# Modulation ahead of the splits, a boundary left to the scheduler, six split chunks, and shorter row steps in a two-block transformer kernel

## The chip, the cores and the metric

The kernel runs on one core of one Trainium2 chip. What counts is the device time of one execution in microseconds. The engines named here are PE (TensorE, the matrix multiplications), ACT (ScalarE), DVE (VectorE), POOL (GpSimd) and SP (SyncE, which here only starts transfers). A kernel is timed in several runs and the median is given; one more execution is recorded by the hardware profiler, and all rows below come from that one.

## The reference

Two networks run one behind the other on a residual stream `x` of 512 tokens by 1024 features, in float32. The first block is an attention mixer of two kinds of heads, a cross attention to a memory of 256 rows, and a SwiGLU MLP. The second has two layers, and its input norms are modulated by a shift and a scale that come from a condition vector:

```python
# block 1
x = x + rms_norm(mixer(rms_norm(x, g_mix_pre)), g_mix_post)
x = x + rms_norm(memory_cross_attention(rms_norm(x, g_mem_pre), m, ...), g_mem_post)
x = x + rms_norm(swiglu(rms_norm(x, g_ffn_pre), w_gate_up, w_down), g_ffn_post)
# block 2: layer 0 has the mLSTM mixer, layer 1 latent attention (MLA)
def modulate(h, shift, scale):
    return h * (1 + scale[:, None, :]) + shift[:, None, :]
def sqrelu_mlp(h, w1, w2):
    return jnp.square(jax.nn.relu(h @ w1)) @ w2
```

Shift, scale and the gates of each layer are rows of the product of the condition vector with a large matrix, `ada_w`; MLA has such rows of its own (`kv_ada_w`). Every norm divides by the root of the mean square over the 1024 features.

## The kernel before

**Products.** Each float32 operand is split into a high and a low part, and a product is three matmuls into the same bank: high by high (L447), high by low (L448) and low by high (L449). Activations are split by `parts` (high on ACT L626, low on DVE L627), weight chunks on ACT L307 or L317 and DVE L308 or L318. A hidden chunk of the relu² MLPs, after the first block of columns, is made with the seven products of Winograd's scheme (`wino`, L510, DVE lines 524 to 534), then goes through relu, square (L1458, L1459) and `parts`.

**Boundaries.** At the end of a stage `boundary` walks over the four token tiles. A tile's product is accumulated (DVE L1358) and multiplied by the gain (L1363), its mean square taken on ACT (L579) and turned into a factor on POOL (`rstd`, L568 and L562), the residual stream updated (DVE L648), its mean square taken again, and the stream scaled for the next stage (`scaled`, ACT L598). `put` then transposes the scaled tile on PE (L608), applies the modulation where there is one (`mod`: two 128x128 pieces of each half on DVE L616, two on ACT L619), and splits. Between these steps the products of the next tiles and, at the end, the first products of the next stage, given by `first`, are issued. The whole is inside `ordered()`, in which PE, ACT, DVE and POOL keep the order of the program text. Outside it a list scheduler with a simulated timeline sets each engine's order; a region can be given a priority (`hot`).

**MLP.** `mlp` goes over blocks of hidden chunks. In the last block it sets a cap of `lc` split weight chunks in advance (`cap`), loads the two weight groups of the block, and leaves its products to `boundary`. Split chunks live in buffers of a pool of `s8` = 14; a buffer comes free when the last product that reads it has run.

**Rows in the background.** A generator makes the modulation rows beside the main work. A half row of 512 columns takes eight loads of 128x512 from `ada_w` (`araw`, POOL L868, four buffers), eight multiply-adds on DVE (L863), one fold (L872), a split, and one matmul with ones that sums over partitions (the row sum, L881). The row is scaled (L898), stored to memory (`arow`, POOL L201) and, as a column, loaded again (`cols_steps`, POOL L381) and transposed on PE (L386). Each step of the generator takes in two loads and issues two. Main work advances it: `step(cost)` takes the cost from a counter, 0.65 for a product, 0.34 for a Winograd product, and when the counter falls below zero it is set to `pace` again and the generator takes one step.

```python
        self.pace -= cost
        if self.pace < 0 and not self.quiet:
            self.pace = BUF["pacb" if self.late else "pace"]
            self.step_bg()
```

**Start.** `self.before` names, by the number of the weight chunk, the loads of x tiles (`get`) that are issued on SP ahead of that chunk's load.

## Time and profile before

| | |
|---|---|
| median of three runs | 2026.44 us (2026.16 to 2029.08) |
| the profiled execution, its own time | 2028.55 us |
| its span | 2026.5 us |
| mean granted TensorE clock | 0.985 |
| PE busy | 1943.2 us (96%), 10738 matmuls |
| DVE busy | 1373.4 us (68%) |
| ACT busy | 1073.1 us (53%) |
| POOL busy | 355.6 us (18%) |
| traffic | 242.01 MB, mean 119 GB/s |

The profiled execution is 2.1 us above the median, and 2.05 us of it lie outside the span. The rows that follow further down come from four views: the waits (who waits for whom, in sum), the timeline of an engine (start, length, engine, line, operation, output and inputs, number of instructions in the row, and in brackets the idle time ahead of it with what ended it), windows (busy time by engine in a stretch, with the granted clock, where 1.00 is 2.4 GHz and 0.50 is 1.2), and the instructions of one line. `L447` is line 447 of the kernel before.

### The profile page before, as it was taken

How to read it: one execution, taken by the hardware profiler on the slowest of the kernel's cores; microseconds unless marked ns; L12 is line 12 of the kernel's file. 1: busy time of each engine (PE TensorE's matmuls, PEld its weight loads, DVE VectorE, ACT ScalarE, POOL GpSimd, SP SyncE). 2: the span in 40 equal slices, each digit the busy share in tenths (PEclk: the TensorE clock that was granted, in tenths of full speed). 3: DMA queues.
4: the chain of work that ended last, by engine and by line, in shares of the span. 5: the costliest groups of instructions: out<-in, count | busy, mean ns of one | idle time of the engine just before them, and what ended most of it. 6: DMA issues, size and time to landing. Idle time of an engine off the chain costs nothing. (4 is left out here: it accounts for less than half of the span.)

```text
span 2026.5 us, 29742 instructions
## 1 busy us (share of the span) xinstructions
PE 1943.2 (96%) x10738; PEld 1663.4 (82%) x10738; DVE 1373.4 (68%) x2689; ACT 1073.1 (53%) x2355; POOL 355.6 (18%) x711
## 2 busy tenths in 40 slices
PE   7999999999999999899999899998889989999997
PEld 5888988878888888678888788888687879989996
DVE  5756655856666665576866888898568747657665
ACT  6767775545353243556446464455465556545543
POOL 1331111201122211121323221222120012000000
PEclk9999999999999999999999999999999999999999
DMA  6322342523465554153442354565243212233321
GB/s 198 89 79 65 113 136 74 187 73 115 136 208 177 161 172 116 52 169 101 154 135 84 110 162 138 185 188 165 62 114 94 84 63 73 73 114 105 104 85 62
DMA packets 175251, 242.01 MB, mean 119 GB/s; under 512 B 20108, under 2 KB 117537, under 8 KB 175105
## 3 DMA queue, kind: packets, MB, share of 16 engines
q1 hardware_dynamic: 150704, 170.53, 27.2%
q0 software_dynamic: 24400, 69.60, 11.5%
q8 instruction: 84, 1.38, 0.3%
q14 instruction: 63, 0.51, 0.1%
HBM read 237.88 MB, written 2.20 MB: 118 GB/s over the span
## 5 line engine op out<-in xcount | busy, mean ns | idle before, releaser
L447 PE MATMUL ps<-s,s 128*128 128x512 f32 (+4 forms) x2276 | 863.0, 381 | 26.7 <-ACT s L626 25.1
L448 PE MATMUL ps<-s,s 128*128 128x512 f32 (+4 forms) x2276 | 851.6, 375 | 2.8 <-DVE s L627 1.9
L449 PE MATMUL ps<-s,s 128*128 128x512 f32 (+4 forms) x2276 | 849.7, 375 | 1.5 <-DVE s L627 1.4
L447 PEld LDWEIGHTS ps<-s,s 128*128 128x128 f32 (+2 forms) x2276 | 432.0, 190 | 105.9 <-ACT s L626 31.0
L449 PEld LDWEIGHTS ps<-s,s 128*128 128x128 f32 (+2 forms) x2276 | 431.2, 190 | 83.2 <-DVE s L627 5.2
L448 PEld LDWEIGHTS ps<-s,s 128*128 128x128 f32 (+2 forms) x2276 | 432.3, 190 | 79.1 <-DVE s L627 4.0
L510 PEld LDWEIGHTS ps<-s,s 128*128 128x128 f32 x2184 | 261.8, 188 | 6.7 <-DVE u L526 4.5
L510 PE MATMUL ps<-s,s 128*128 128x256 f32 x2184 | 263.7, 281 | 3.6 <-DVE u L526 3.6
L307 ACT ACTIVATE s<-raw 128x512 fp32r<-128x512 f32 x277 | 157.8, 622 | 143.2 <-PE ps L449 97.9
L308 DVE TENSOR_TENSOR s<-raw,s 128x512 fp32r<-128x512 f32 x277 | 190.3, 726 | 57.0 <-ACT s L307 55.7
L863 DVE SCALAR_TENSOR_TENSOR u<-araw,cond,u 128x512 f32<-128x512 f32 x224 | 167.3, 747 | 24.2 <-DMA araw<-in_ada_w 15.4
L317 ACT ACTIVATE s<-raw,cols_all 128x256 fp32r<-128x256 f32 (+1 forms) x305 | 143.5, 546 | 66.5 <-PE ps L449 29.8
L318 DVE SCALAR_TENSOR_TENSOR s<-raw,cols_all,s 128x256 fp32r<-128x256 f32 (+1 forms) x305 | 147.6, 538 | 39.3 <-ACT s L317 38.7
L868 POOL DMA_DIRECT2D araw<-in_ada_w x192 | 104.0, 542 | 338.0 <-DVE u L863 289.2
L627 DVE TENSOR_TENSOR s<-u,s 128x512 fp32r<-128x512 f32 x126 | 87.0, 700 | 79.4 <-ACT s L626 56.7
L626 ACT ACTIVATE s<-u 128x512 fp32r<-128x512 f32 x126 | 77.6, 625 | 63.8 <-PE ps L449 31.9
L568 POOL TENSOR_SCALAR sm<-sm,sm 128x1 f32<-128x1 f32 x34 | 10.5, 307 | 527.5 <-ACT junk L579 527.4
L341 ACT ACTIVATE s<-raw 128x512 fp32r<-128x512 f32 x104 | 62.7, 621 | 72.7 <-PE ps L449 37.6
L627 DVE TENSOR_TENSOR s<-ps,s 128x512 fp32r<-128x512 f32 (+3 forms) x100 | 59.1, 606 | 42.4 <-ACT s L626 35.0
L341 ACT ACTIVATE s<-u 128x512 fp32r<-128x512 f32 x78 | 48.7, 624 | 66.8 <-DVE u L345 36.4
L342 DVE TENSOR_TENSOR s<-raw,s 128x512 fp32r<-128x512 f32 x104 | 70.7, 683 | 15.4 <-ACT s L341 15.1
L1358 DVE TENSOR_TENSOR u<-ps,u 128x512 f32<-128x512 f32 x80 | 53.9, 685 | 34.3 <-PE ps L449 33.6
(261 smaller groups left out, 2162.9 us busy)
## 6 DMA issues: line engine op xcount, KB each, us to landing
raw<-in_mlp_w SPq DMA_DIRECT2D x128, 512.0 KB, 3.8
araw<-in_ada_w POOLq DMA_DIRECT2D x192, 256.0 KB, 3.5
raw<-in_w_gate_up SPq DMA_DIRECT2D x44, 512.0 KB, 4.1
raw<-in_w_in SPq DMA_DIRECT2D x24, 512.0 KB, 4.2
raw<-in_a_w_in SPq DMA_DIRECT2D x24, 512.0 KB, 3.8
raw<-in_w_down SPq DMA_DIRECT2D x22, 512.0 KB, 3.7
raw<-in_w_mem_kv SPq DMA_DIRECT2D x16, 512.0 KB, 3.6
araw<-in_kv_ada_w POOLq DMA_DIRECT2D x32, 256.0 KB, 4.0
```

What stands on the lines that cost most here:

```text
L307: A.activation(hi[:, sl, cl], src[:, sl, cl], AF.Copy)
L308: f.tensor_tensor(out=lo[:, sl, cl], in0=src[:, sl, cl], in1=hi[:, sl, cl].bitcast(F32), op=ALU.subtract)
L317: A.activation(hi[:, i, :], src[:, i, :], AF.Copy, scale=g)
L318: V.scalar_tensor_tensor(out=lo[:, i, :], in0=src[:, i, :], scalar=g, in1=hi[:, i, :].bitcast(F32), op0=ALU.mult, op1=ALU.subtract)
L341: A.activation(hi, x, AF.Copy)
L447: self.nc.tensor.matmul(ps, lhsT=ah, rhs=bh, start=first and i == 0, stop=False)
L448: self.nc.tensor.matmul(ps, lhsT=ah, rhs=bl, start=False, stop=False)
L449: self.nc.tensor.matmul(ps, lhsT=al, rhs=bh, start=False, stop=last and i == n - 1)
L510: nc.tensor.matmul(ps, lhsT=l[:, k, :], rhs=m[:, k, :], start=first and k == e == 0, stop=k == 3 and e == 2, skip_group_check=True)
L627: self.nc.vector.tensor_tensor(out=lo, in0=x, in1=hi.bitcast(F32), op=ALU.subtract)
L863: V.scalar_tensor_tensor(out=acc, in0=raws.pop(j), scalar=vec[:, j:j + 1], in1=acc, op0=ALU.mult, op1=ALU.add)
L868: nc.gpsimd.dma_start(out=raws[j], in_=ws[:, j, :])
```

## The change

Six things are edited. In `put`, with a modulation, both halves of a tile are modulated first, in place of the scaled tile, and then both are split. `boundary` gets an argument `fixed`; without it the region isn't held in program order, and the scalings, puts and reductions run with the scheduler's priority `hb` = 300. The first relu² MLP, in front of MLA, uses `fixed=False`; the last MLP, which has no next stage, stays. `lc` goes from 7 to 6, `pace` and `pacb` from 2.0 to 1.9. A column is transposed five generator steps after its load instead of three. At the start the x tiles are loaded before weight chunks 1 and 3 instead of 2 and 4.

```diff
-BUF = dict(... pace=2.0, pacb=2.0, ... lc=7, ...)
+BUF = dict(... pace=1.9, pacb=1.9, ... lc=6, ...)
...
-        for _ in range(3):
+        for _ in range(5):
             yield None
...
     def put(self, ys, h, k, t, mod=None):
+        todo = []
         for y, cw in ys:
...
-            hi, lo = h.blk(k, n, tt(t))
             if mod:
                 g, sh = mod
-                y = self.u2((P, n, P))
+                y = y.rearrange("p (n c) -> p n c", c=P)
...
                 ps = y
+            todo.append((k, n, ps))
+            k += n
+        for k, n, ps in todo:
+            hi, lo = h.blk(k, n, tt(t))
             self.parts(hi, lo, ps)
-            k += n
...
-    def boundary(self, y_of, nxt, first, late=(1, 1, 2)):
+    def boundary(self, y_of, nxt, first, late=(1, 1, 2), fixed=True):
...
-        with self.ordered():
+        hot = nullcontext if fixed else lambda: self.hot("hb")
+        with self.ordered() if fixed else nullcontext():
...
-                    if n == 4 and nxt and t >= 2:
+                    if n == 4 and nxt and t >= 2 and fixed:
                         self.put(*pend.pop(t - 2))
-                if nxt and t >= 1:
-                    scaled(t - 1)
-                rs[t] = a(t, ys, ss)
+                with hot():
+                    if nxt and t >= 2 and not fixed:
+                        self.put(*pend.pop(t - 2))
+                    if nxt and t >= 1:
+                        scaled(t - 1)
+                    rs[t] = a(t, ys, ss)
             if nxt:
-                i = -1
+                if not fixed:
+                    with hot():
+                        scaled(NT - 1)
                 for i, need in enumerate(first):
-                    if i == late[0]:
+                    if fixed and i == late[0]:
                         scaled(NT - 1)
-                    for n, t in ((1, NT - 2), (2, NT - 1)):
-                        if i == late[n]:
-                            self.put(*pend.pop(t))
+                    for t in sorted(pend):
+                        if t <= need if not fixed else i >= late[t - 1]:
+                            with hot():
+                                self.put(*pend.pop(t))
...
-        self.before = {2: [lambda: get(1)], 4: [lambda: get(2), lambda: get(3)], 6: [biases]}
+        self.before = {1: [lambda: get(1)], 3: [lambda: get(2), lambda: get(3)], 6: [biases]}
...
-    def mlp(self, blocks, up, w_down, g, nxt, first, ready=None, caps=None):
+    def mlp(self, blocks, up, w_down, g, nxt, first, ready=None, caps=None, fixed=True):
...
-                self.boundary(y_of, nxt, first)
+                self.boundary(y_of, nxt, first, fixed=fixed)
...
-        self.mlp(BUF['mb'], up, self.a["mlp_w2_2"][l], g, nxt, first, ready, BUF['mc'])
+        self.mlp(BUF['mb'], up, self.a["mlp_w2_2"][l], g, nxt, first, ready, BUF['mc'], fixed=nxt is None)
```

How this moves instructions, at three places. In the rows a name ends in two numbers, the buffer and the tile's own number, and from `boundary` on the lines of the changed kernel are a few higher (L608 becomes L609, L626 L629, L881 L891).

The first place is PE at the end of the first relu² MLP's Winograd products. Before, `ps_14007` is the first tile's product of the last block, `s_2498_13975` its last hidden chunk, and `ps_13831` and `ps_13833` belong to the last Winograd products:

```order
L448 MATMUL ps_14007<-s_2489_13903,s_2453_13669 128x512
L510 MATMUL ps_13831<-s_2021_10571,s_2473_13795 128x256 x12
L449 MATMUL ps_14007<-s_2489_13903,s_2454_13670 128x512
L510 MATMUL ps_13833<-s_2064_10938,s_2474_13814 128x256 x12
L447 MATMUL ps_14007<-s_2493_13942,s_2498_13975 128x512
L448 MATMUL ps_14007<-s_2493_13942,s_2498_13975 128x512
L449 MATMUL ps_14007<-s_2493_13942,s_2498_13975 128x512
```

With the change, `ps_14094`, `ps_14119`, `ps_14157` are products of the last block (two tiles, two column halves), `ps_13946` belongs to the last Winograd product, and the last hidden chunk, `s_2520_14073`, is first used 17 matmuls after this `L510` row:

```order
L449 MATMUL ps_14157<-s_2510_13975,s_2486_13801 128x512
L447 MATMUL ps_14157<-s_2514_14010,s_2485_13800 128x512
L510 MATMUL ps_13946<-s_2106_11099,s_2500_13927 128x256 x12
L449 MATMUL ps_14094<-s_2514_14010,s_2486_13801 128x512
L447 MATMUL ps_14094<-s_2514_14010,s_2485_13800 128x512
L448 MATMUL ps_14094<-s_2514_14010,s_2485_13800 128x512
L448 MATMUL ps_14119<-s_2518_14063,s_2485_13800 128x512
L449 MATMUL ps_14119<-s_2518_14063,s_2486_13801 128x512
L449 MATMUL ps_14094<-s_2514_14010,s_2486_13801 128x512
L447 MATMUL ps_14119<-s_2518_14063,s_2485_13800 128x512
L448 MATMUL ps_14119<-s_2518_14063,s_2485_13800 128x512
L449 MATMUL ps_14119<-s_2518_14063,s_2486_13801 128x512
```

The four products of the first two tiles now stand among and behind the last Winograd matmuls, where one product stood.

The second place is the boundary of that MLP with MLA, on ACT. `x_10_91` and `x_11_92` are the third and the fourth tile of the residual stream, and `u_2589_14368` (before) and `u_2611_14458` (after) the first MLA tile. Before:

```order
L598 ACTIVATE u_2575_14308<-x_10_91,sm_14220 128x512
L598 ACTIVATE u_2576_14310<-x_10_91,sm_14220 128x512
L579 ACTIVATE junk_14319,sm_14318<-x_11_92 128x1024
L317 ACTIVATE s_2562_14261<-raw_13994,cols_2283_12462 128x384
L317 ACTIVATE s_2568_14279<-raw_14003,cols_2283_12462 128x384 x2
L317 ACTIVATE s_2569_14288<-raw_14264,cols_2283_12462 128x384
L579 ACTIVATE junk_14371,sm_14370<-u_2589_14368 128x256
L598 ACTIVATE u_2594_14377<-u_2589_14368,sm_14375 128x256
L598 ACTIVATE u_2598_14389<-x_11_92,sm_14323 128x512
L598 ACTIVATE u_2599_14391<-x_11_92,sm_14323 128x512
L626 ACTIVATE s_2537_14155<-ps_14393 128x4x128
```

With the change:

```order
L598 ACTIVATE u_2595_14395<-x_10_91,sm_14307 128x512
L598 ACTIVATE u_2596_14397<-x_10_91,sm_14307 128x512
L317 ACTIVATE s_2589_14374<-raw_14372,cols_2123_11223 128x384 x2
L317 ACTIVATE s_2647_14622<-raw_14437,cols_2123_11223 128x384 x2
L317 ACTIVATE s_2649_14639<-raw_14455,cols_all_1926 128x512 x2
L579 ACTIVATE junk_14406,sm_14405<-x_11_92 128x1024
L629 ACTIVATE s_2565_14284<-ps_14538 128x4x128
L629 ACTIVATE s_2567_14288<-ps_14543 128x4x128
L317 ACTIVATE s_2650_14648<-raw_14496,cols_all_1926 128x512 x2
L598 ACTIVATE u_2603_14412<-x_11_92,sm_14410 128x512
L598 ACTIVATE u_2604_14414<-x_11_92,sm_14410 128x512
L579 ACTIVATE junk_14461,sm_14460<-u_2611_14458 128x256
```

The two scalings of `x_11_92` stood behind the mean square of the MLA tile and stand ahead of it now. On POOL `row_14325` is the MLA bias row that DVE's L1693 adds to that tile, and `sm_14323` the factor of `x_11_92`; before:

```order
L568 TENSOR_SCALAR sm_14312<-sm_14267,sm_14303 128x1
L562 TENSOR_TENSOR sm_14314<-sm_14312,mhalf_80 128x1
L568 TENSOR_SCALAR sm_14321<-sm_14318 128x1
L562 TENSOR_TENSOR sm_14323<-sm_14321,mhalf_80 128x1
L585 DMA row_14325<-arow_4175 128x320
L585 DMA row_14583<-arow_4175 128x384
L568 TENSOR_SCALAR sm_14373<-sm_14370 128x1
```

With the change the load, now `row_14416`, is in the boundary behind the mLSTM mixer:

```order
L562 TENSOR_TENSOR sm_10540<-sm_10538,mhalf_80 128x1
L568 TENSOR_SCALAR sm_10614<-sm_10374,sm_10605 128x1
L562 TENSOR_TENSOR sm_10616<-sm_10614,mhalf_80 128x1
L585 DMA row_14416<-arow_4175 128x320
L568 TENSOR_SCALAR sm_10623<-sm_10620 128x1
L562 TENSOR_TENSOR sm_10625<-sm_10623,mhalf_80 128x1
```

It moved by 110 places of POOL's order, out of the MLA boundary.

The third place is PE in the first block of the first relu² MLP, where `u_2055_10873` (before) and `u_2121_11174` (after) are the row loaded back as a column. Before:

```order
L448 MATMUL ps_10803<-s_2021_10571,s_1989_10414 128x256
L449 MATMUL ps_10803<-s_2021_10571,s_1989_10414 128x256
L881 MATMUL ps_10855<-u_2052_10828,onesr_78 128x512
L386 MATMUL ps_10911<-ident_66,u_2055_10873 128x8
L447 MATMUL ps_10979<-s_1995_10449,s_2044_10785 128x512
L448 MATMUL ps_10979<-s_1995_10449,s_2044_10785 128x512
```

With the change:

```order
L448 MATMUL ps_11142<-s_2035_10600,s_2079_10923 128x512
L449 MATMUL ps_11142<-s_2035_10600,s_2080_10924 128x512
L891 MATMUL ps_11159<-u_2099_11079,onesr_78 128x512
L447 MATMUL ps_11143<-s_2034_10591,s_2079_10923 128x512
...
L448 MATMUL ps_11143<-s_2062_10825,s_2102_11090 128x512
L449 MATMUL ps_11143<-s_2062_10825,s_2102_11090 128x512
L386 MATMUL ps_11221<-ident_66,u_2121_11174 128x8
L447 MATMUL ps_11239<-s_2063_10842,s_2079_10923 128x512
L448 MATMUL ps_11239<-s_2063_10842,s_2079_10923 128x512
```

Between the row sum and the transposition stood nothing, and now 36 matmuls stand there.

## Rows read from the trace of the kernel before

**Rows 1.** Waits of PE: engine, line, releaser: us in total, times, longest.

```profile
PE ps L447 <- ACT s L626: 25.1, 16, 3.9
PE ps L608 <- ACT u L598: 18.3, 10, 7.5
PE ps L386 <- DMA u<-arow: 5.8, 2, 4.7
PE ps L1824 <- DVE u L1833: 4.9, 3, 2.5
```

**Rows 2.** Timeline of PE, last block, first relu² MLP: start us, us, [idle <-releaser].

```profile
1407.22 0.50 PE L881 MATMUL ps<-u,onesr 128*128 128x512 f32 x1 [3.64 <-DVE u L627]
...
1416.59 0.50 PE L447 MATMUL ps<-s,s 128*128 128x512 f32 x1 [1.70 <-ACT s L626]
...
1421.21 0.79 PE L447 MATMUL ps<-s,s 128*128 128x512 f32 x1 [3.25 <-ACT s L626]
...
1423.84 0.80 PE L449 MATMUL ps<-s,s 128*128 128x512 f32 x1 [1.41 <-DVE s L627]
```

**Rows 3.** Timeline of POOL, DVE, ACT, PE at the boundary behind that MLP.

```profile
1466.00 1.16 POOL L585 DMA_DIRECT2D row<-arow  x2
1471.07 0.49 DVE L1693 TENSOR_TENSOR u<-ps,row 128x320 f32<-128x320 f32 x1 [3.21 <-DMA row<-arow]
1473.57 1.32 ACT L598 ACTIVATE u<-x,sm 128x512 f32<-128x512 f32 x2
1474.33 1.97 PE L608 MATMUL ps<-ident,u 128*128 128x128 f32 x8 [7.50 <-ACT u L598]
```

**Rows 4.** Timeline of PE around a row sum in that MLP's first block.

```profile
1115.74 0.50 PE L881 MATMUL ps<-u,onesr 128*128 128x512 f32 x1 [0.81 <-DVE u L627]
1120.94 0.27 PE L386 MATMUL ps<-ident,u 8*128 8x8 f32 x1 [4.70 <-DMA u<-arow]
```

**Rows 5.** Timeline of DVE, then of PE, at the SwiGLU boundary.

```profile
831.88 0.69 DVE L627 TENSOR_TENSOR s<-u,s 128x512 fp32r<-128x512 f32 x1 [2.67 <-PE ps L449]
835.98 1.27 PE L608 MATMUL ps<-ident,u 128*128 128x128 f32 x8 [2.80 <-ACT u L598]
```

**Rows 6.** Windows: stretch, us, busy us (instructions) per engine, PEclk, DMA share, GB/s.

```profile
470.00:870.00 400.00, 392.68 (x1795) 320.41 (x1794) 255.39 (x453) 163.14 (x341) 75.68 (x149) 1.00 0.46 145
```

**Rows 7.** Windows on the nine stretches of lower clock, and their sum.

```profile
1117.52:1124.35 6.83, 3.41 (x9) 2.71 (x10) 6.69 (x12) 1.26 (x2) 1.28 (x3) 0.50 0.01 1
...
1417.89:1428.13 10.24, 5.58 (x13) 3.92 (x13) 7.96 (x14) 3.96 (x9) 1.61 (x3) 0.50 0.77 231
1469.09:1479.33 10.24, 5.00 (x21) 5.01 (x22) 5.45 (x19) 5.23 (x12) 0.78 (x2) 0.50 0.59 136
...
sum 54.61, PE 39.37 PEld 33.22 DVE 39.27 ACT 27.30 POOL 5.42; mean PE 4.37 PEld 3.69 DVE 4.36 ACT 3.03 POOL 0.60
```

**Rows 8.** Timeline of ACT in the stretch of rows 2.

```profile
1418.52 1.46 ACT L317 ACTIVATE s<-raw,cols 128x320 fp32r<-128x320 f32 x3
```

**Rows 9.** Windows, line 863 on DVE alone, 1376 to 1427 us: DVE busy (instructions).

```profile
1376.00:1427.00 51.00, 11.93 (x16) 0.88 0.63 191
```

**Rows 10.** Timeline of PE, last block of the second relu² MLP.

```profile
1987.29 0.50 PE L447 MATMUL ps<-s,s 128*128 128x512 f32 x1 [2.04 <-ACT s L626]
```

**Rows 11.** Timeline of PE at the start of the program.

```profile
29.59 0.80 PE L447 MATMUL ps<-s,s 128*128 128x512 f32 x1 [3.88 <-ACT s L626]
```

**Rows 12.** Timeline of ACT in a put at the SwiGLU boundary.

```profile
841.04 0.80 ACT L619 ACTIVATE u<-ps,cols,cols 128x128 f32<-128x128 f32 x2 [1.46 <-DVE u L616]
```

**Rows 13.** Line 863: idle time of DVE before it; the page's loads for it.

```profile
  DMA araw<-in_ada_w: 15.4, 18
...
araw<-in_ada_w POOLq DMA_DIRECT2D x192, 256.0 KB, 3.5
```

**Rows 14.** The page's section 6, loads of MLP weights: KB each, us to landing.

```profile
raw<-in_mlp_w SPq DMA_DIRECT2D x128, 512.0 KB, 3.8
...
raw<-in_w_gate_up SPq DMA_DIRECT2D x44, 512.0 KB, 4.1
```

More of the change, by code (lines that the diff above doesn't have):

```diff
@@ L32 @@
 ALL = slice(0, S)
-BUF = dict(s8=14, u2=15, row=2, raw=4, w0=4, w1=4, w2=4, w3=5, w4=5, w5=5, w6=5, w7=5, ps=8, pace=2.0, pacb=2.0, man=0, lag=3, lagx=3, lagm=3, half=1, quiet=1, xp=0, fp=2, r1=1.25, r1b=3.6, r1c=2.4, r2=1.6, r2b=2.6, rx=1.4, rm=0.6, pre=10, gl=3, pl=0, hb=300, hs=0, ha=0, sp=0, spq=1.3, sq=1, b1=1, b2=1, lc=7, ar=4, mb=(6, 8, 6, 6, 6), mc=(4, 3, 4, 4, 4), st2=1, pr2=8, z1=4.5, z2=5, gt=3, rv=2, gs=1, rl=3, n1=4, ex=2, em=3, vg=1, sb=(8, 8, 6), mo=4, x1=2, g0=20, st=1, y1=0, y2=1, y3=0, ph=0, pq=0, fy=1, u1=6, s32=4, sm=60)
+BUF = dict(s8=14, u2=15, row=2, raw=4, w0=4, w1=4, w2=4, w3=5, w4=5, w5=5, w6=5, w7=5, ps=8, pace=1.9, pacb=1.9, man=0, lag=3, lagx=3, lagm=3, half=1, quiet=1, xp=0, fp=2, r1=1.25, r1b=3.6, r1c=2.4, r2=1.6, r2b=2.6, rx=1.4, rm=0.6, pre=10, gl=3, pl=0, hb=300, hs=0, ha=0, sp=0, spq=1.3, sq=1, b1=1, b2=1, lc=6, ar=4, mb=(6, 8, 6, 6, 6), mc=(4, 3, 4, 4, 4), st2=1, pr2=8, z1=4.5, z2=5, gt=3, rv=2, gs=1, rl=3, n1=4, ex=2, em=3, vg=1, sb=(8, 8, 6), mo=4, x1=2, g0=20, st=1, y1=0, y2=1, y3=0, ph=0, pq=0, fy=1, u1=6, s32=4, sm=60)
 TWO_PI = 2.0 * np.pi
```

## The prediction

> **What bounds the kernel now.** TensorE (PE) does, through the time in which it waits and the time in which it runs slowly after a wait. I read the view of PE's waits first: the three largest causes are the products that wait for a high half of a split on ACT, the transposes that wait for the scaled residual stream on ACT, and a column of a modulation row that waits for a DMA [rows 1]. Then I asked where on the timeline these waits lie, because the same wait may be spread thinly or sit in one place. They are bunched: four waits at the last block of the first relu² MLP (1407 to 1424 us) [rows 2], one of 7.50 us at the boundary behind it [rows 3], one of 4.70 us in the first block of that MLP [rows 4], one of 2.80 us at the SwiGLU boundary [rows 5]. In between PE is full: from 470 to 870 us it is busy for 392.68 of 400 us although DVE works 255.39 us of them [rows 6]. Third, the windows with a granted clock of 0.50, that is 1.2 instead of 2.4 GHz: nine stretches, each behind or around such a wait, with 39.37 us of PE work in them [rows 7]; half of that, 19.7 us, is what the low clock costs. So a wait of some us is paid for twice, and I charge each stall with its idle time and half of the PE work of its slow stretch. The number of matmuls is the same before and after, so only these losses can change, and new ones come.
>
> **The change part by part.**
>
> *A, last block of the first relu² MLP.* Three edits meet here: `lc` 7 to 6, the shorter row step, and the products left to the scheduler. Before, PE idles 3.64 us for the row sum's operand, then 1.70, 3.25 and 1.41 us for the last hidden chunk [rows 2]: 10.0 us, and the slow stretch from 1417.89 holds 5.58 us of work [rows 7], 2.8 more: 12.8. Two things delay that chunk. ACT splits three 320-wide weight chunks of the next stage for 1.46 us in front of it [rows 8], which are the seventh chunk that `lc` = 6 does not admit; and DVE has 16 row products, 11.93 us, in that 51 us stretch [rows 9]. After, steps come sooner and the row work ends ahead of the last block: in PE's order the last row sum stands before that block's first Winograd matmul, where five sums stood behind that point. And 17 matmuls, at 392.68/1795 = 0.22 us [rows 6] some 4 us, stand between the last Winograd matmul and the first use of the last hidden chunk, where one stood before. What is left I read off the kernel's last MLP, whose last block has neither row work nor a next stage: 2.04 us at its last chunk [rows 10], with a little slow clock 3.5. Gain 9 (6 to 12).
>
> *B, the MLA boundary.* The chain reads backwards from the PE wait [rows 3]: the transposes of the fourth tile wait 7.50 us for ACT's scaling, which began at 1473.57; ACT stood behind a mean square of the first MLA tile, that one behind DVE's bias add at 1471.07, which waited 3.21 us for a row load; and POOL issued that load at 1466.00, as two loads behind the boundary's own reductions. The scaling needed none of this: only program order put it there. Slow clock adds half of 5.00 us [rows 7], 2.5: 10.0 in all. After, POOL's order has the load in the boundary behind the mLSTM mixer, hundreds of us earlier, and ACT's order has the two scalings ahead of the MLA mean square. New on ACT in front of them: the splits of put(2)'s tile, which wait for its transposes, and two 512-wide weight splits. From the start of put(2)'s transposes to that of put(3)'s I count transposes 1.27 [rows 5], then two splits, two weight splits and a scaling at 0.66 each, half of the pair of scalings [rows 3]: 4.6 us, against PE's transposes and 14 matmuls of 320 columns at 0.14 between them, 3.2; a wait of 1.4, with the second half and some slow clock 3. Gain 7; bounds 10 (no wait is left) and 0 (the wait is only renamed, below).
>
> *C, the column later.* Before, PE's next instruction after the row sum at 1115.74 is the transposition that needs the row stored and loaded back, and it waits 4.70 us [rows 4]; all such waits together are 5.8 [rows 1], the row sum's own 0.81, and half of 3.41 us of slow work 1.7 [rows 7]: 8.3. With five steps instead of three, 36 matmuls stand between the two, 36 x 0.22 = 7.9 us against a chain of 5.2 (1115.74 to 1120.94). So the DMA is hidden; I leave 1.3 for the row sum itself. Gain 7 (5 to 8). Readers of that column are later too, but it belongs to a later stage.
>
> *D, attention of MLA.* Waits of PE for DVE's scaled probabilities are 4.9 us [rows 1], and row products lie between DVE's instructions there; the rows are done before, so those 0.75 us pieces go. Gain 3.5 with the slow clock (0 to 6).
>
> *E, the SwiGLU boundary.* PE waits 2.80 us for a scaling; DVE's low split at 831.88 had waited 2.67 us for a weight buffer that a product of the fourth tile frees [rows 5], and the accumulation of the third tile queued behind it. That split belongs to the seventh chunk; with six it takes a free buffer. But one chunk is split later. Gain 2.5 (0 to 4).
>
> *F, the start.* Loads of x one chunk earlier: the wait of 3.88 us [rows 11] stands behind eight weight splits on ACT, and now x tile 1 lands earlier but w's second chunk later, on the same SP queue. Gain 1 (-4 to 5).
>
> *G, both halves' modulations first.* A put takes ACT's two modulations 0.80 us behind a 1.46 us wait for DVE's two, twice [rows 12]; after, the four modulations run back to back and the second half's splits are ready about 1.6 us sooner, the first half's 0.8 later. PE waits for the first half behind the mLSTM mixer and for the second elsewhere: 0 (-3 to +3). The modulation in place costs no instruction.
>
> *H, row steps more often.* A product counts 0.65 against a pace of 2.0: a step after every fourth product, now (1.9 - 3 x 0.65 < 0) after every third; a Winograd product counts 0.34 and stays at every sixth. Total row work is unchanged, but 22 row sums instead of 18 lie before 1156 us. Four half rows of eight products at 0.75 us [rows 9] are 24 us of DVE brought into some 790 us. DVE already waits 15.4 us in 18 places for row loads [rows 13]. A load has two steps' time to land, before 4 x 3 x 0.22 x 2 = 5.3 us, now 4.0; it needs 3.5 to land [rows 13] plus 0.75 to 1.5 us of buffer release. So waits appear in the denser stretches. Cost 3 (0 to 10): DVE has a third of its time free there, and PE has shown no wait for it. The Trainium skill, page "DMA: Bandwidth & Descriptors", section "Issuing engines are not separate DMA queues", speaks against this part: transfers that different engines start interleave on the same 16 DMA engines, so row loads would delay weights. Here weights land in 4.1 us in the SwiGLU MLP, beside rows, and in 3.8 in the relu² MLPs, of which the second has no rows [rows 14], so the trace shows at most 0.3 us of it for a load. By that rule, with nothing hidden, the 44 loads of the SwiGLU MLP would lose 13 us and the sum would end near 2012; by the trace, in whose view of waits no product waits for a weight's DMA [rows 1], it stays.
>
> **Sum.** -9 - 7 - 7 - 3.5 - 2.5 - 1 + 0 + 3 = -27. Against the profiled execution, 2028.55, this is 2001.5; the median, 2026.44, is 2.1 lower: 1999.4, and I say 1999.
>
> **The rivals.** *Rows too dense (slower).* Steps in pairs take two products 1.5, two issues 1.1 and 3.5 of landing, 6.1 us, against 4.0 to 4.2 us that two steps now last. If DVE stands at the load each time, with weight splits and splits of activations queued behind it, that is 1.9 us in each of about 56 pairs, 106 us of DVE time; half of it reaching PE gives 1999 - 3 + 53 = 2049. It turns slower than before when more than 30 us of the 106 reach PE. For it: 18 such waits exist. Against it: PE hardly waits in the 400 us of [rows 6], in the middle of the time in which row products run [rows 13]. The interleaving that the skill's page states would feed the same mechanism.
> *The boundary's wait only changes its name.* Six to eight weight splits of 0.6 us stand on ACT between the third and the fourth tile's scaling; if one waits for a buffer that a late product frees, B gains nothing: 1999 + 7 = 2006; with the slow clock 2008.
> *The last block keeps its stall.* If the hidden chunk's own chain (add, two activations, two splits, about 3 us) and not the other work set it, A gains 2: 2006.
> *The denser rows take back about two thirds*: 18 us more: 2017, or all: no difference.
> *Everything goes well*: A 12, B 10, E 4, F 4, H 0: about 1985.
>
> **How the numbers follow.** Forecast 1999, with its own bounds 1990 to 2008: 0.55. Better, about 1985 to 1990: 0.12. The boundary's wait renamed 0.11, the last block's stall kept 0.08, both near 2006 to 2010. Rows take back two thirds 0.05, all 0.03. Slower, about 2049: 0.06. The range 1984 to 2014 leaves out the last three and little else. A difference below 0.2% (4 us) can't be told from none: faster 0.91, same 0.03, slower 0.06.
>
> **What would show it.** Right: no PE wait above 3 us at the fourth tile of the MLA boundary and ACT's scaling ahead of the MLA mean square; no row product in the last 50 us of the first relu² MLP; the transposition behind the row sum without a DMA wait; five or fewer stretches at 0.50. Wrong: more and longer waits of DVE for row loads between 365 and 1060 us with PE waits behind them, or ACT's weight splits waiting for PE at the MLA boundary.

## The result and the profile after

The changed kernel took 2006.55 us (median of four runs, 2005.94 to 2008.94) against 2027.67 for the kernel before on the same chip (four runs). The ratio is 0.9898 with a 95% interval of 0.9881 to 0.9915: 1.0% faster, 21 us. Forecast was 1999 with a range of 1984 to 2014. The profiled execution has a span of 2005.4 us; PE is busy 1937.4 us of it and the mean granted clock is 0.986. The time came in near the forecast, but not by the forecast's route: the stretches up to 1393 us came out 24 us worse than forecast, those behind them 19 us better, so that the near fit of the sum is in good part luck.

Where the time went is best seen by the start of the same-numbered PE matmul in both traces (10,696 of them, row sums and columns left out; this is called the numbering below). In the table the first column is the time in the trace before; the second is how far the changed kernel is ahead (-) or behind (+) there.

| time before, us | changed minus before, us | what lies in the stretch that ends here |
|---|---|---|
| 794.0 | +0.1 | start, first block's mixers, SwiGLU |
| 869.7 | -2.6 | SwiGLU boundary |
| 892.9 | +4.9 | start of the mLSTM mixer |
| 1076.4 | +6.6 | mLSTM mixer and its boundary |
| 1146.8 | +15.3 | first block of the first relu² MLP |
| 1393.1 | +17.0 | its Winograd blocks |
| 1441.9 | +1.8 | its last block |
| 1487.9 | -7.3 | boundary with MLA |
| 1550.4 | -13.3 | start of the MLA attention |
| 1632.2 | -14.3 | rest of the attention |
| 1722.0 | -20.9 | behind the attention, start of the second relu² MLP |
| 2018.8 | -21.1 | second relu² MLP |

The view of PE's waits (engine and line, releaser: us in total, times, longest) of the changed kernel:

```profile
PE ps L447 <- ACT s L629: 19.0, 11, 3.3
PE ps L891 <- DVE u L630: 11.0, 2, 6.6
PE ps L386 <- DMA u<-arow: 5.9, 1, 5.9
...
PE ps L609 <- ACT u L598: 3.8, 3, 2.8
PE ps L1834 <- DVE u L1843: 0.9, 2, 0.6
```

Against [rows 1], the products' wait for ACT's high halves fell from 25.1 to 19.0 us, the transposes' wait for the scaling (now L609) from 18.3 to 3.8 and the attention's (now L1834) from 4.9 to 0.9. The column's wait for its DMA is as large as before, now in a single place, and the row sum (now L891) stands second: it waits 11.0 us in two places, once 6.6, where the view of the kernel before has 4.8 us in three:

```profile
PE ps L881 <- DVE u L627: 4.8, 3, 3.6
```

The windows of lower clock hold 42.80 us of PE work, more than the 39.37 of [rows 7], and are nine as before:

```profile
1130.32:1140.56 10.24, 5.92 (x14) 4.69 (x15) 9.90 (x11) 1.26 (x2) 4.39 (x6) 0.50 0.01 2
...
sum 51.20, PE 42.80 PEld 35.88 DVE 42.24 ACT 21.00 POOL 15.45; mean PE 4.76 PEld 3.99 DVE 4.69 ACT 2.33 POOL 1.72
```

The last block, now at 1410 to 1444 us, has no wait left. From 1376 to 1427 us, the times of [rows 9], PE is busy throughout, and no row product is there; the last one is at 1351 us (windows: stretch, its length, busy us and instructions by engine, granted clock, DMA share, GB/s):

```profile
1376.00:1427.00 51.00, 51.00 (x347) 47.08 (x346) 36.14 (x64) 27.69 (x53) 0.00 (x0) 1.00 0.34 107
```

At the boundary with MLA no transposition waits any more. POOL issues the bias row's load at 1084.55, and on ACT the scaling of the fourth tile stands ahead of the MLA mean square, as the order had it. What is left are two waits of PE for the splits of the third tile, 2.7 us in all. ACT's rows, then PE's:

```profile
1471.13 1.32 ACT L598 ACTIVATE u<-x,sm 128x512 f32<-128x512 f32 x2
1472.36 0.40 ACT L579 ACTIVATE junk<-u 128x256 bf16<-128x256 f32 x1
```
```profile
1468.31 0.42 PE L447 MATMUL ps<-s,s 128*128 128x320 f32 x1 [1.80 <-ACT s L629]
...
1469.77 0.41 PE L449 MATMUL ps<-s,s 128*128 128x320 f32 x1 [0.90 <-DVE s L630]
```

The new loss is in the first block of the first relu² MLP. The timeline rows of POOL, DVE and PE, in order of time:

```profile
1115.09 0.49 POOL L201 DMA_DIRECT2D arow<-u  x1 [25.08 <-DVE u L908]
...
1123.29 9.94 POOL L482 TENSOR_TENSOR u<-s 128x512 f32<-128x512 f32 x8
```
```profile
1123.18 10.60 DVE L345 TENSOR_TENSOR u<-raw,raw 128x512 f32<-128x512 f32 x1
1133.81 0.69 DVE L630 TENSOR_TENSOR u<-u,u 64x512 fp32r<-64x512 f32 x1
...
1147.50 0.67 DVE L908 SCALAR_TENSOR_TENSOR u<-ps,u 1x512 f32<-1x512 f32 x1
```
```profile
1148.46 0.49 POOL L201 DMA_DIRECT2D arow<-u  x1 [7.94 <-DVE u L908]
1150.29 0.52 POOL L381 DMA_DIRECT2D u<-arow  x1 [1.34 <-DMA arow<-u]
```
```profile
1134.64 0.77 PE L891 MATMUL ps<-u,onesr 128*128 128x512 f32 x1 [6.64 <-DVE u L630]
...
1152.06 0.24 PE L386 MATMUL ps<-ident,u 8*128 8x8 f32 x1 [5.87 <-DMA u<-arow]
```

Read from the end: the column's transposition at 1152.06 waits 5.87 us for a load that POOL issued at 1150.29, behind the store at 1148.46, which had waited for DVE's L908 (the row's scaling, L898 before) at 1147.50. The DMA is not what is late: 4.6 us from L908 to the transposition, against 12.1 us between the row sum's end (1135.4) and L908. DVE was behind by then, because one addition of two weight quarters, L345, stood from 1123.18 for 10.60 us, which otherwise takes 0.69. In just this time POOL ran the eight additions of L482 (high plus low halves of the stream, for Winograd's sums) without a break. And POOL had them all in one stretch because it stood at a row's store for 25.08 us first and then issued eight row loads, with L482 queued behind. Before, only one short load of the row work (0.60 us) stood ahead of them, and they began as their operands came:

```profile
1089.32 2.57 POOL L482 TENSOR_TENSOR u<-s 128x512 f32<-128x512 f32 x2 [4.76 <-PE ps L608]
1095.52 1.31 POOL L482 TENSOR_TENSOR u<-s 128x512 f32<-128x512 f32 x1 [3.63 <-DVE s L627]
1098.38 5.11 POOL L482 TENSOR_TENSOR u<-s 128x512 f32<-128x512 f32 x3 [1.56 <-DVE s L627]
1111.72 3.42 POOL L482 TENSOR_TENSOR u<-s 128x512 f32<-128x512 f32 x2 [8.22 <-DVE s L627]
```

### The profile page after: what moved, and what is told of

It is laid out like the page before. It is cut to its first block, busy times and chain, and to the rows that moved or that the text cites. A ratio compares the mean times of both kernels' runs of the same rounds, so it can differ in the third digit from the quotient of the medians.

```text
span 2005.4 us, 29787 instructions
## 1 busy us (share of the span) xinstructions
PE 1937.4 (97%) x10738; PEld 1663.3 (83%) x10738; DVE 1379.5 (69%) x2689; ACT 1068.4 (53%) x2355; POOL 358.4 (18%) x711
## 4 chain that ended last, share of the span: by engine, by line
PE 82%; DVE 8%; issue 4%; ACT 4%; DMA 1%; POOL 1%; SPq 0%; DVEq 0%; POOLq 0%; ACTq 0%
PE ps L447 21%; PE ps L449 21%; PE ps L448 20%; PE ps L510 11%; PE ps L1033 1%; DVE s L318 1%; PE ps L609 1%; PE ps L1823 1%; PE ps L1852 1%; PE ps L1004 1%; PE ps L1583 1%; DVE s L342 1%; DVE s L630 1%; PE ps L1017 1%; DVE u L345 1%
## 5 line engine op out<-in xcount | busy, mean ns | idle before, releaser
L510 PEld LDWEIGHTS ps<-s,s 128*128 128x128 f32 x2184 | 262.6, 189 | 9.9 <-ACT u L530 4.5
L510 PE MATMUL ps<-s,s 128*128 128x256 f32 x2184 | 264.4, 281 | 6.6 <-ACT u L530 4.3
L308 DVE TENSOR_TENSOR s<-raw,s 128x512 fp32r<-128x512 f32 x277 | 188.9, 719 | 64.1 <-ACT s L307 62.8
L873 DVE SCALAR_TENSOR_TENSOR u<-araw,cond,u 128x512 f32<-128x512 f32 x224 | 168.2, 751 | 19.6 <-DMA araw<-in_ada_w 13.3
L318 DVE SCALAR_TENSOR_TENSOR s<-raw,cols_all,s 128x256 fp32r<-128x256 f32 (+1 forms) x305 | 147.3, 538 | 33.7 <-ACT s L317 33.1
L630 DVE TENSOR_TENSOR s<-u,s 128x512 fp32r<-128x512 f32 x126 | 84.6, 687 | 66.3 <-ACT s L629 45.1
L629 ACT ACTIVATE s<-u 128x512 fp32r<-128x512 f32 x126 | 76.2, 627 | 67.7 <-PE ps L449 26.2
L630 DVE TENSOR_TENSOR s<-ps,s 128x512 fp32r<-128x512 f32 (+3 forms) x100 | 59.5, 607 | 37.8 <-ACT s L629 30.2
```

Of the source, the lines that this page charges most:

```text
L308: f.tensor_tensor(out=lo[:, sl, cl], in0=src[:, sl, cl], in1=hi[:, sl, cl].bitcast(F32), op=ALU.subtract)
L318: V.scalar_tensor_tensor(out=lo[:, i, :], in0=src[:, i, :], scalar=g, in1=hi[:, i, :].bitcast(F32), op0=ALU.mult, op1=ALU.subtract)
L510: nc.tensor.matmul(ps, lhsT=l[:, k, :], rhs=m[:, k, :], start=first and k == e == 0, stop=k == 3 and e == 2, skip_group_check=True)
L630: self.nc.vector.tensor_tensor(out=lo, in0=x, in1=hi.bitcast(F32), op=ALU.subtract)
L873: V.scalar_tensor_tensor(out=acc, in0=raws.pop(j), scalar=vec[:, j:j + 1], in1=acc, op0=ALU.mult, op1=ALU.add)
```

## The experiments

The ratio is to the kernel before, run beside each; us differences are between medians, with the changed kernel at 2006.55. The kernel before had medians from 2025.28 to 2027.67 in these runs, so a difference of 2 to 3 us between two of them is hardly more than noise.

**The boundary held in program order again.**

```diff
-        self.mlp(..., BUF['mc'], fixed=nxt is None)
+        self.mlp(..., BUF['mc'])
```

> The changed kernel, with the boundary between the first relu² MLP and MLA held in program order again; all else as changed. Theory (the free order alone took the stall away): the transposes of the fourth tile wait some 7 us again for ACT's scaling behind the MLA mean square, with the slow clock behind it; 9 us slower than the changed kernel, about 2015 us (2012 to 2018). Rival (six chunks or the earlier row load would have done it): no wait over 3 us there, 2005 to 2008 us.

Measured: 2022.47 us, ratio 0.9979 (0.9970 to 0.9988); 16 us slower than the changed kernel, beyond the theory's 2018. PE's rows from the last block to the boundary, then the rows of POOL, DVE and ACT there:

```profile
1427.55 0.50 PE L447 MATMUL ps<-s,s 128*128 128x512 f32 x1 [0.77 <-ACT s L629]
...
1430.81 0.50 PE L447 MATMUL ps<-s,s 128*128 128x512 f32 x1 [2.04 <-ACT s L629]
...
1472.82 0.64 PE L447 MATMUL ps<-s,s 128*128 128x320 f32 x1 [5.05 <-ACT s L317]
```
```profile
1473.22 1.18 POOL L585 DMA_DIRECT2D row<-arow  x2
```
```profile
1478.03 0.49 DVE L1703 TENSOR_TENSOR u<-ps,row 128x320 f32<-128x320 f32 x1 [3.12 <-DMA row<-arow]
```
```profile
1480.54 1.32 ACT L598 ACTIVATE u<-x,sm 128x512 f32<-128x512 f32 x2
```

The chain of [rows 3] is back link by link: the two row loads on POOL, DVE's bias add that waits 3.12 us for them, and the fourth tile's scaling 7 us after the load's issue. But PE spends the time in another place than expected. PE waits 5.05 us for a split of MLA's weights ahead of the third tile's transposes, so that the fourth tile's wait only 0.89. That six chunks put this split so late is likely, but no run with a fixed order and seven chunks beside the other edits shows it. The last block, without row work and with its order fixed, keeps waits of 0.77 and 2.04 us, the numbers of the last MLP [rows 10]; the free order removes these too. By the numbering of matmuls the stretch up to 1441.9 gives 10.2 us instead of 15.2, and the one up to 1487.9 gives 0 instead of 9.1.

**The free boundary alone, on the kernel before.**

```diff
...
-                self.boundary(y_of, nxt, first)
+                self.boundary(y_of, nxt, first, fixed=fixed)
...
```

With it goes all that the change does inside `boundary`.

> The kernel before with one edit of the change alone: the boundary between the first relu² MLP and MLA left to the scheduler (seven chunks, old row step, old column step, old start, old put). Theory (the free order by itself removes the boundary's 7.5 us and fills most of the last block's waits with other tiles' products): both stretches lose under 4 us together instead of 25, the mLSTM part and the attention stay as before: about 2012 us (2008 to 2017). Rival (the row work must be gone from the last block first): 2020 us or more.

Measured: 2017.29 us, ratio 0.9949 (0.9934 to 0.9964): the gain is 9 us, just outside the theory's range. Three of PE's waits from 1400 to 1480 us:

```profile
1406.86 0.50 PE L888 MATMUL ps<-u,onesr 128*128 128x512 f32 x1 [3.64 <-DVE u L627]
...
1439.91 1.27 PE L608 MATMUL ps<-ident,u 128*128 128x128 f32 x8 [3.17 <-ACT u L598]
...
1470.30 0.41 PE L447 MATMUL ps<-s,s 128*128 128x320 f32 x1 [1.95 <-ACT s L626]
```

The fourth tile's 7.50 us of [rows 3] and the last hidden chunk's waits of [rows 2] are gone, and the row sum in the last block (3.64) stays. But the first tile's transposes now wait 3.17 us, and products wait for splits of the later tiles in four places, 6.4 us together: the two stretches still idle 13.2 us, where the theory had less than 4. The edit gives 9 us alone (10.6 by the numbering, over the two stretches) and 16 together with the others (14.1): the rows' work and the free order share these two stretches.

**The old row step in the changed kernel.**

```diff
-BUF = dict(... pace=1.9, pacb=1.9, ...)
+BUF = dict(... pace=2.0, pacb=2.0, ...)
```

> The changed kernel with the row step at 2.0 again. Theory (the new waits at 892, 1134 and 1152 us come from the denser rows, which put eight row loads ahead of the eight additions of L482 on POOL, so that these run in one stretch and keep DVE's L345 for 10.6 us): L345 there lasts under 2 us, the row sum's wait of 6.64 us is gone, and so is the one at 892 us; in exchange row products lie in the last block and in the attention again. About -20 and +12: 1998 us (1993 to 2008). Rival (the later column set that order): the waits stay and the row work in the last block comes on top: 2015 us or more.

Measured: 2011.44 us, ratio 0.9927 (0.9912 to 0.9942), 5 us slower than the changed kernel; neither number was hit, and the theory is only half right. The waits at 892 and 1152 us are gone, and at the matmul that stood at 1393 us before, this kernel is 7.3 us ahead of the kernel before where the changed one is 17.0 behind. But the long DVE instruction is there all the same, and a row sum waits again:

```profile
1104.17 10.82 DVE L630 TENSOR_TENSOR s<-u,s 128x512 fp32r<-128x512 f32 x1
```
```profile
1131.47 0.77 PE L891 MATMUL ps<-u,onesr 128*128 128x512 f32 x1 [9.68 <-DVE u L630]
```
```profile
1431.93 1.95 PE L609 MATMUL ps<-ident,u 128*128 128x128 f32 x8 [4.92 <-ACT u L598]
```
```profile
1646.86 0.45 PE L447 MATMUL ps<-s,s 128*128 128x256 f32 x1 [4.71 <-ACT s L629]
```

L630 stands for 10.82 us beside the eight additions, and the row sum, whose own split DVE reaches late, waits 9.68. POOL had waited 26.00 us at a row load this time. So it is not the density of the rows alone that puts the additions in one stretch; a row step that waits ahead of them on POOL will do. The stand is there in every run that takes back a single one of the six edits (10.57 to 10.82 us), and not in the kernel before with the free boundary: which edits together bring it is open. After 1400 us the old step gives everything back: PE waits 4.92 us at the boundary and 4.71 behind the attention. By the numbering the shorter step costs 24 us up to 1393 and returns 28 after it.

**Three column steps again.**

```diff
-        for _ in range(5):
+        for _ in range(3):
             yield None
```

> The changed kernel with three steps ahead of the column's transposition instead of five. Theory (the denser rows are the cause): POOL's order still has eight loads and then eight additions, DVE's L345 still stands for 10 us, the row sum still waits over 5 us; 2003 to 2012 us. Rival (the later column is the cause, or the wait of 5.87 us is its own): the wait for the column is 4 to 6 us as before, but the row sum's is under 1 us: 1998 us or less.

Measured: 1999.97 us, ratio 0.9868 (0.9853 to 0.9883): 6.6 us faster than the changed kernel, between the two theories. The row sum waits as predicted by the first (6.82), DVE's L345 stands 10.57 us, and no column waits more than 0.38 us for a DMA:

```profile
1117.47 10.57 DVE L345 TENSOR_TENSOR u<-raw,raw 128x512 f32<-128x512 f32 x1
```
```profile
1128.91 0.76 PE L891 MATMUL ps<-u,onesr 128*128 128x512 f32 x1 [6.82 <-DVE u L630]
...
1159.29 0.50 PE L891 MATMUL ps<-u,onesr 128*128 128x512 f32 x1 [2.50 <-DVE u L630]
```

So the later column, meant to hide the store and load, cost 6.6 us. What it does besides is to shift the phase of all later row steps: behind the late row sum at 1128.91 no column follows any more (the transpositions next to it are at 1093 and 1212 us), the wait of the row sum near 890 us is 2.77 instead of 4.37 and a wait of 4.34 in a Winograd product at 1356 us is missing, while new waits of row sums of 2.50, 1.86 and 2.18 come. Which of these belongs to the column and which to the shifted phase is not settled by this run.

**The additions on DVE.**

```diff
-                G.tensor_tensor(out=x, in0=hi[:, k].bitcast(F32), in1=lo[:, k].bitcast(F32), op=ALU.add)
+                V.tensor_tensor(out=x, in0=hi[:, k].bitcast(F32), in1=lo[:, k].bitcast(F32), op=ALU.add)
```

> The changed kernel with the additions of L482 (eight in each relu² MLP) on DVE instead of POOL. Theory (POOL's additions hold DVE's second operand back): L345 falls from 10.6 to 0.7 us and DVE spends 8 x 0.69 = 5.5 us on the additions, so the row sum's wait falls from 6.64 to about 2 us and what follows comes 4 to 5 us earlier; 16 additions cost DVE 11 us, mostly beside PE: about 2000 us (1996 to 2004). Rival (L345 is long for another reason, a late operand): it stays near 10 us and the added DVE work comes on top, 2008 to 2013 us.

Measured: 1993.40 us, ratio 0.9836 (0.9819 to 0.9852): 13 us faster than the changed kernel, more than the theory's range allows. DVE does the eight additions in 4.91 us and L345 takes its usual time:

```profile
1120.90 4.91 DVE L482 TENSOR_TENSOR u<-s 128x512 f32<-128x512 f32 x8
1125.72 0.68 DVE L345 TENSOR_TENSOR u<-raw,raw 128x512 f32<-128x512 f32 x1
```

The waits of 6.64 and 5.87 us are both gone, though the column still has its five steps and the rows their density. In the numbering the stretch up to 1146.8 us costs -9 instead of +9 us.

**Half of them on DVE.**

```diff
-            for x, (hi, lo) in zip(f, q):
-                G.tensor_tensor(out=x, ...)
+            for e, x, (hi, lo) in zip((V, V, G, G), f, q):
+                e.tensor_tensor(out=x, ...)
```

> The changed kernel with half of the L482 additions on DVE and half on POOL. Theory (a DVE instruction with two operands in SBUF can be kept out for as long as POOL runs additions without a break): the longest DVE instruction at that place lasts 5 to 6 us, four additions of 1.25, instead of 10.6; the row sum's wait is 2 to 5 us; 1994 to 2003 us, between the versions with all of them on POOL (2006.5) and on DVE (1993.4). Rival (POOL lets DVE in between two additions): no DVE instruction above 2 us and 1992 to 1995 us.

Measured: 1998.59 us, ratio 0.9863 (0.9846 to 0.9879). As the theory has it:

```profile
1121.98 7.61 DVE L482 TENSOR_TENSOR u<-s 128x512 f32<-128x512 f32 x4
```
```profile
1122.09 5.14 POOL L482 TENSOR_TENSOR u<-s 128x512 f32<-128x512 f32 x4
```
```profile
1131.05 0.47 PE L891 MATMUL ps<-u,onesr 128*128 128x512 f32 x1 [2.88 <-DVE u L630]
...
1141.46 0.20 PE L386 MATMUL ps<-ident,u 8*128 8x8 f32 x1 [1.40 <-DMA u<-arow]
```

Of the 7.61 us of the four DVE additions in the first row the first takes 5.80, the time of four POOL additions and its own 0.68, and the two waits are 2.88 and 1.40 us, about a half and a quarter of what they were. The stand of DVE at this place goes with the number of POOL's additions: 10.6 for eight, 5.8 for four, none for none.

**The additions on DVE, in the kernel before.** The edit of L482 alone:

```diff
-                G.tensor_tensor(out=x, ...)
+                V.tensor_tensor(out=x, ...)
```

> The kernel before with L482 on DVE, nothing else. Theory (the long stand of DVE is new with the change: before, the additions start as their operands come, and DVE's instructions beside them last 1.8 instead of 0.7 us, five of them in the first relu² MLP): a gain of 1 to 6 us at most, 2020 to 2026 us. Rival (the additions on POOL cost the kernel before as much as the changed one): about 13 us less, 2013 us.

Measured: 2024.26 us, ratio 0.9987 (0.9977 to 0.9997), a gain of 2.6 us, as the theory has it. So some 10 of the 13 us are a loss that the change brought.

**Seven chunks again.**

```diff
-BUF = dict(... lc=6, ...)
+BUF = dict(... lc=7, ...)
```

> The changed kernel with seven chunks in an MLP's last block again. Theory (six chunks shorten the SwiGLU boundary, whose later waits at 846 to 862 us are gone in the changed kernel, and matter little at the MLA boundary with its free order): 3 to 5 us come back between 835 and 865 us, at the MLA boundary 0 to 2: about 2011 us (2008 to 2014). Rival (those waits went with put, not with the chunks): 2005 to 2008 us.

Measured: 2016.52 us, ratio 0.9954 (0.9939 to 0.9969), 10 us slower than the changed kernel, beyond the theory's 2014. By the numbering 2.6 us come back at the SwiGLU boundary and 4.4 at the MLA boundary, where PE waits for the splits of a later tile:

```profile
1473.78 0.63 PE L447 MATMUL ps<-s,s 128*128 128x320 f32 x1 [1.05 <-ACT s L629]
...
1476.01 0.64 PE L449 MATMUL ps<-s,s 128*128 128x320 f32 x1 [1.33 <-DVE s L630]
```

The rest is spread over steps of under 2 us.

**The old put.** Each half is modulated, into a tile of its own, and split before the next, as in the kernel before.

```diff
+            hi, lo = h.blk(k, n, tt(t))
             if mod:
...
-                y = y.rearrange("p (n c) -> p n c", c=P)
+                y = self.u2((P, n, P))
...
-            todo.append((k, n, ps))
+            self.parts(hi, lo, ps)
             k += n
-        for k, n, ps in todo:
-            hi, lo = h.blk(k, n, tt(t))
-            self.parts(hi, lo, ps)
```

> The changed kernel with the old put, where each half of a tile is modulated and split in turn. Theory (what the changed kernel gained behind the MLA attention and in the SwiGLU boundary comes from the missing row work and the six chunks): within 2 us, 2005 to 2009 us. Rival (modulating both halves first did it): the waits at 846 to 862 us and the second waits behind MLA come back, 2011 us or more.

Measured: 2015.34 us, ratio 0.9945 (0.9930 to 0.9959), 9 us slower: the rival by its time. Of its sign little is there: three waits for the scaling that the changed kernel doesn't have (0.61 us at 851, 0.83 at 1075 and at 1648 us), and longer stretches of low clock behind the same 3.1 us wait. They don't add up to 9 us; by the numbering the loss comes in steps of 1 to 3 us all along the kernel, and its cause stays open.

**The old start.**

```diff
-        self.before = {1: [lambda: get(1)], 3: [lambda: get(2), lambda: get(3)], 6: [biases]}
+        self.before = {2: [lambda: get(1)], 4: [lambda: get(2), lambda: get(3)], 6: [biases]}
```

> The changed kernel with x loaded ahead of weight chunks 2 and 4 again at the start. Theory (the start is worth what the first hundred products show, 0.8 us): within 2 us of the changed kernel, 2005 to 2009 us. Rival (the earlier loads of x cost the weights' arrival): 2004 us or less.

Measured: 2009.10 us, ratio 0.9919 (0.9904 to 0.9934): 2.6 us slower by the medians, at the edge of the expected band; the two ratios' intervals overlap, so it is not clear of noise. The first hundred matmuls are 1.45 us later than in the changed kernel.

**Both repairs in the changed kernel.**

```diff
-        for _ in range(5):
+        for _ in range(3):
...
-                G.tensor_tensor(out=x, ...)
+                V.tensor_tensor(out=x, ...)
```

> The changed kernel with L482 on DVE and with three column steps: both repairs at once. Theory (both act on the same two waits at 1134 and 1152 us, and the three steps beyond them only on the one at 892 us and some small ones): not the sum of 13 and 6.5 us but 13 to 16 below the changed kernel, 1990 to 1994 us. Rival (they are separate losses): the sum, about 1987 us or less.

Measured: 1988.18 us, ratio 0.9810 (0.9793 to 0.9826), 18 us faster than the changed kernel and nearly the sum of 13 and 6.6: the rival, or close to it. So three column steps are worth 5 us even where the two waits are gone.

**And a longer row step from the mLSTM mixer's end on, with both repairs kept.**

```diff
-BUF = dict(... pace=1.9, pacb=1.9, ...)
+BUF = dict(... pace=1.9, pacb=2.3, ...)
```

> L482 on DVE and three column steps as in the run that took 1988.2 us, and the row step at 2.3 instead of 1.9 from the mLSTM mixer's end on. Theory (rows are now too dense in the first relu² MLP, where PE waits 4.8 and 2.2 us for row sums, and still end before its last block): both waits under 2 us, 1980 to 1987 us. Rival (a row sum waits for DVE however dense the rows are): one such wait of 3 us or more stays, 1986 to 1992 us.

Measured: 1982.62 us, ratio 0.9790 (0.9776 to 0.9805), the best of all: 2.1% faster than the kernel before, in the theory's range. The waits of the row sums fall from 10.6 us in total (first row, both repairs) to 5.0 (second row), though the two that are left, of 2.8 and 2.2 us, are longer than the theory's 2:

```profile
PE ps L891 <- DVE u L630: 10.6, 5, 4.8
```
```profile
PE ps L891 <- DVE u L630: 5.0, 2, 2.8
```

## Why the prediction was right in sum and wrong in its parts

The sum was -27 and the result -21; the parts, measured by the numbering of matmuls, were these. In the stretches from 870 to 1393 us, in which C and H lie, -4 was forecast and +19.6 measured; A, B, D and the stretch behind the attention (G) came out 18.4 us better than forecast. That the two nearly cancel is luck. Of the four signs of being right two came (no wait above 3 us at the MLA boundary's fourth tile, with the scaling ahead of the MLA mean square, and no row product in the last 50 us of the MLP), and two did not: the transposition behind the row sum waits 5.87 us for a DMA, and there are nine stretches of low clock instead of five or fewer.

- **A, last block**: -9 forecast, -15.2 measured. Two sizes were off. The loss before is larger than the 12.8 us: behind the row sum's wait lies a further slow stretch (windows), whose 3.41 us of work add half, 1.7, to make 14.5:

```profile
1407.65:1411.06 3.41, 3.41 (x10) 2.63 (x9) 2.69 (x6) 0.47 (x2) 0.59 (x2) 0.50 0.51 137
```

  And the remainder of 3.5 us, read off the last MLP, is nothing. It is right for a block whose order is fixed (0.77 and 2.04 us in the run with the fixed boundary), but products of other tiles now stand among the Winograd matmuls and fill these too. I had counted the 17 matmuls and not used them.
- **B, MLA boundary**: -7 forecast, -9.1 measured, and the mechanism is the forecast one: the scaling ahead of the mean square, the row's load early. Of the remaining wait of 3 us 2.7 came, as two waits for the third tile's splits; of the 2.1 us more, 1.3 is a wait of the third tile's transposes before, which the sum left out. The free order doesn't do this by itself: alone it gives 1.1 us in this stretch.
- **C, the column**: -7 forecast. The 4.70 us of [rows 4] did go, but a wait of 5.87 us stands behind a later row sum, and the kernel is 6.6 us faster without the edit. The step that failed set 36 matmuls, 7.9 us, against a chain of 5.2 us that began with the row sum. The store, the load and their issue still take 4.6 us, but between the row sum and the row's scaling on DVE lie 12.1 us, since DVE was late and its order had other work there. Where DVE is in time the step holds: with the additions on DVE the scaling starts 2.4 us behind the row sum, and 30 matmuls cover the chain. A chain's length read in one place holds only as long as nothing stands in its queues.
- **D, attention**: -3.5 forecast, -6.0 and -1.0 measured in its two stretches; the row products are gone and the wait is 0.9 us where [rows 1] have 4.9. With the old row step the two stretches give -2.4 and -0.3, so most of it is the rows', as forecast.
- **E, SwiGLU boundary**: -2.5 forecast and -2.7 measured, but not by the named cause; that the numbers agree is luck. DVE's split waits 2.75 us as before and PE 2.80:

```profile
833.39 0.69 DVE L630 TENSOR_TENSOR s<-u,s 128x512 fp32r<-128x512 f32 x1 [2.75 <-PE ps L449]
```
```profile
837.49 1.97 PE L609 MATMUL ps<-ident,u 128*128 128x128 f32 x8 [2.80 <-ACT u L598]
```

  The row of [rows 5] was misread: its line, L627, splits activations in `put`, not weight chunks (L308, L318), so it never belonged to the seventh chunk. What went are the waits after it, at 846 to 862 us, of which [rows 5] shows nothing; with seven chunks 2.6 us come back there, a wait of 1.39 among them.
- **F, start**: -1 forecast; -0.8 in the first hundred matmuls, none of it left at 794 us; 2.6 us by the run with the old start, which is not clear of noise.
- **G, put**: 0 forecast, 9 us by the run with the old form, from a cause that stays open. The gain behind the attention, -6.6 us, hangs on two edits: it is -3.7 with the old put, and +3.2 with the old row step. The bounds of 3 us either way were too narrow.
- **H, denser rows**: +3 forecast. Its price up to 1393 us is 24 us by the run with the old step: 7.5 at the mLSTM mixer's start, where a row sum waits 4.37 us for its split while DVE works off the mixer's gates ahead of it, 7 of the +8.7 in the MLP's first block, and steps of 2 to 3 us elsewhere.

```profile
892.11 0.76 PE L891 MATMUL ps<-u,onesr 128*128 128x512 f32 x1 [4.37 <-DVE u L630]
```

  The step that failed is that DVE, with a third of its time free, would not make PE wait; both large waits of the row sum are for a split that DVE reached late. I had looked for the price in row products and at the DMAs, where the trace shows little: DVE's waits for row loads fell from 15.4 to 13.3 us, and row loads land in 3.4 instead of 3.5 us [rows 13]. I didn't look at POOL's queue, which the steps were moved past: eight additions stood behind a row's store there. That stand is not H's alone, as the old row step has it too. In exchange the last row product is at 1351 us, against 1670 with the old step, and without that A, B, D and G give 27 us less.

The rival of rows that are too dense was right that the price is queueing behind rows, but wrong in the queue and far off in size. Loads of the SwiGLU weights land in 4.6 us in the changed kernel against 4.1 before [rows 14], and in 4.4 with the old row step; at 794 us the changed kernel is level with the one before, so that this cost nothing to speak of. The rule of the Trainium skill, page "DMA: Bandwidth & Descriptors", section "Issuing engines are not separate DMA queues", that transfers interleave whoever starts them, may stand behind these tenths, but no run here shows a loss by it.

## What to carry to other kernels

When background work is moved in time, go through every queue that it is issued on and see what it now stands ahead of; POOL, busy for 18% of the span, cost some 10 us that way here. A chain that is covered by so many matmuls is only covered if each engine on it is free to take it up, so measure from the place where the last engine is late. And undo each part alone: a sum that fits can hide one part that costs as much as another gains. What a part is worth alone need not be what it is worth beside the others, as the free boundary shows with 9 and 16 us.

## What the runs showed of the hardware

A DVE instruction with two operands in SBUF can be kept out for as long as POOL runs additions that read SBUF: 10.60 us beside eight of them (1.25 to 1.31 us each), 5.80 beside four, 0.68 without. In other places of the same traces the two engines alternate: in the kernel before, DVE's splits beside the same additions last 1.8 instead of 0.69 us and POOL's additions 1.7 instead of 1.28. Two of DVE's rows there, of which three of the four and one of the three instructions last 1.8:

```profile
1098.22 5.83 DVE L308 TENSOR_TENSOR s<-raw,s 128x512 fp32r<-128x512 f32 x4
...
1110.95 3.02 DVE L627 TENSOR_TENSOR s<-u,s 128x512 fp32r<-128x512 f32 x3 [3.20 <-PE ps L449]
```

The Trainium skill, page "SBUF — State Buffer", section "Who interferes with whom", states that a DVE instruction with two SBUF inputs contends with a GpSimd instruction that reads SBUF, and that what they share is an exclusive lock. The traces agree that DVE blocks, and show that it can stay blocked over several POOL instructions in a row.

What decides between the two patterns is not settled. It is not the instruction: L627, which alternates above, is L630 in the run with the old row step and stands there for 10.82 us. Nor is it the moment: the stands shown above begin 0.1 to 0.2 us before POOL's stretch (1123.18 against 1123.29), but in the second relu² MLP of that run one of 7.44 us begins in the middle of a stretch, and lasts to its end. DVE's row, then POOL's:

```profile
1688.32 7.44 DVE L630 TENSOR_TENSOR s<-u,s 128x512 fp32r<-128x512 f32 x1 [7.67 <-ACT s L629]
```
```profile
1685.06 10.15 POOL L482 TENSOR_TENSOR u<-s 128x512 f32<-128x512 f32 x8
```

Nor does an unbroken stretch suffice: in the changed kernel's second relu² MLP six additions run without a break beside DVE's L308 at 1668 us, and there the two engines alternate.
